# Small tiles in a pool of their own, ahead of the large ones, in a two-layer hybrid decoder

## The chip, the core and the metric

The kernel runs on one core of one Trainium2 chip. The time is the device time of one execution in microseconds (us). Beside the unprofiled runs there is one profiled execution, from which all views of the trace come. TensorE (PE) multiplies matrices and has a weight-load side of its own (PEld); VectorE (DVE), ScalarE (ACT) and GpSimd (POOL) do elementwise work; SyncE (SP) issues all DMAs. SBUF is the on-chip memory in which all operands lie; a tile has the same start address in each of its 128 partitions, and that start, in bytes, is what this case is about.

## The reference

Two decoder layers over x of 1024 positions x 1024 channels, float32. Cut to what matters:

```python
h = rms_norm(x, pre_mix_norm)
proj = h @ w_in                       # 1024 x 3206
o_diff = diff_attention(rope(dq), rope(dk), dv, lam)   # 4 heads, dense causal
o_dil = dilated_attention(rope(lq), rope(lk), lv)      # 6 heads, 3 dilated patterns
o_ssd = ssd_mixer(z, silu(conv4(xbc)), dt, ...)        # 6 heads, chunked scan
x = x + rms_norm(concat(o_diff, o_dil, o_ssd) @ w_out, post_mix_norm)
h = rms_norm(x, pre_ffn_norm)
u = causal_dwconv(h @ ffn_up, width 3)                 # 1024 x 5632
g, val = split(u)
x = x + rms_norm((silu(g) * val) @ ffn_down, post_ffn_norm)
lam = exp(sum(l0 * l1)) - exp(sum(l2 * l3)) + lambda_init   # one number a layer
```

## The kernel before

All large products are made in three passes of a reduced fp32 form (fp32r): each operand is split into a high part and a low part, and high x high, high x low and low x high are added up in PSUM. Positions are taken in two halves T of 512. Every dense matmul has a stationary operand of 128 x 128 and a moving operand of 128 x 512, so 512 columns stream through the array for each.

There are two ways round:

- `mm3` (lines 203, 206, 207): the weights are stationary (a 128-column slice of `wh` or `wl`, the high and low part of a weight tile) and the activations move (a 512-column slice of `ah` or `al`, the high and low part of the normalised input). It makes the input projection by channel and the FFN's up-projection. 1952 matmuls a line.
- `tm3` (lines 153, 156, 157): the activations are stationary and the weights move. They are `ah`/`al` in the token-major input projection and the output projection (512 a line), and the gated FFN tiles tagged `g` in the down-projection (704 a line).

`wsplit` (line 128) loads a weight tile `wr` by DMA, POOL makes `wh` from it (line 134) and DVE makes `wl` (line 135). PSUM results are moved out by ACT and DVE (conv at 359 and 361, FFN gate 812 to 820, sums 840). Attention (score line 593, transposes 733, values 743) and the SSD scan are woven between the dense matmuls; a scheduler lays each engine's order down from the order of the code and the priorities in `weave` and `follow`.

SBUF tiles come from pools, which are laid behind one another; within a pool, the slots of each tag lie in the order in which the tags are first used. Before, there is `cp` (constants `kc` and `gtr`) and one pool `sp` for everything else. A few small tiles (`cstate` of 112 bytes, `ustate` of 352) come first in `sp`, more of them (`tiny`, `rs_m`, `cs`, `sm`, `nA`, `lt`, `wd`) stand between the large ones, and each shifts what follows. At the start of a layer `layer_constants` (line 300) loads small parameters and works out lambda with a handful of tiny instructions (lines 312 to 320).

Of the kernel before, what the change touches and what calls it, by code (L numbers as in the profile page):

```python
# [22 lines left out]
KT = 8  # L23
# [34 lines left out]

C_GPRE, C_GFFN, C_GOUT = 0, 8, 16
C_SSD = 24  # L60
C_FFN = C_SSD + 35
C_TOT = C_FFN + 176
# [7 lines left out]
def body(ctx, tc, x_in, win, wtm, wdt, wout, wup, wdn, cst, gains, dtb, alog, lamp, kst, rope, out):  # L70
    nc = tc.nc
    P = 128
    cp = ctx.enter_context(tc.tile_pool(name="cp", bufs=1))
    sp = ctx.enter_context(tc.tile_pool(name="sp", bufs=2))
    ps = ctx.enter_context(tc.tile_pool(name="ps", bufs=2, space=PSUM))
    dp = ctx.enter_context(tc.tile_pool(name="dp", bufs=2, space=DRAM))

    V, A, G, T_, Y = nc.vector, nc.scalar, nc.gpsimd, nc.tensor, nc.sync

    kc = cp.tile([P, K_GT], F32, name="kc")  # L80
    gtr = cp.tile([P, P], F32R, name="gtr")
    ident = kc[:, K_ID:K_ID + P]
    tri = kc[:, K_TRI:K_TRI + P]
    gts = gtr[:].bitcast(F32)
    sel = kc[:, K_SEL:K_SEL + 8]
# [16 lines left out]
    def tiny(n=4):  # L102
        return sp.tile([P, 8], F32, tag="tiny", bufs=18, name="tiny")

# [3 lines left out]
    def rstd(ssq, n, scale, eps):  # L108
        m = sp.tile([P, 8], F32, tag="rs_m", bufs=4, name="rs_m")
        r = sp.tile([P, 8], F32, tag="rs_r", bufs=4, name="rs_r")  # L110
        m2 = sp.tile([P, 8], F32, tag="rs_2", bufs=4, name="rs_2")
        q = sp.tile([P, 8], F32, tag="rs_q", bufs=4, name="rs_q")
# [184 lines left out]
    for l in range(NL):  # L297
        lam_init = 0.8 - 0.6 * math.exp(-0.3 * l)
        def layer_constants():
            cs = sp.tile([P, C_TOT], F32, tag="cs", bufs=1, name="cs")  # L300
            Y.dma_start(cs[:], cst[l])
            sw = cs[:, C_SSD:C_SSD + 35].rearrange("p (j c) -> p j c", j=7)
            fw = cs[:, C_FFN:C_FFN + 176].rearrange("p (j c) -> p j c", j=44)
            V.tensor_scalar(cs[:, C_SSD:C_SSD + 35], cs[:, C_SSD:C_SSD + 35], 0.5, None, op0=ALU.mult)
            V.tensor_scalar(cs[:, C_FFN:C_FFN + 88], cs[:, C_FFN:C_FFN + 88], 0.5, None, op0=ALU.mult)
            V.tensor_scalar(cs[:, C_GOUT:C_GOUT + 2], cs[:, C_GOUT:C_GOUT + 2], 1.0 - lam_init, None, op0=ALU.mult)
            sm = sp.tile([P, 182], F32, tag="sm", bufs=1, name="sm")
            Y.dma_start(sm[:, 0:24], dtb[l])
            Y.dma_start(sm[:, 24:48], alog[l])
            Y.dma_start(sm[:, 48:182], lamp[l])  # L310
            nA = sp.tile([P, 24], F32, tag="nA", bufs=1, name="nA")
            A.activation(nA[:], sm[:, 24:48], AF.Exp)
            V.tensor_scalar(nA[:], nA[:], -1.0, None, op0=ALU.mult)
            lt = sp.tile([P, 72], F32, tag="lt", bufs=1, name="lt")
            lv = sm[:, 48:176].rearrange("p (a b d) -> p a b d", a=2, b=2)
            V.tensor_tensor(lt[:, 0:64].rearrange("p (a d) -> p a d", a=2), lv[:, :, 0], lv[:, :, 1], op=ALU.mult)
            V.tensor_reduce(lt[:, 64:66], lt[:, 0:64].rearrange("p (a d) -> p a d", a=2), axis=AX.X, op=ALU.add)
            A.activation(lt[:, 66:68], lt[:, 64:66], AF.Exp)
            V.tensor_tensor(lt[:, 68:69], lt[:, 67:68], lt[:, 66:67], op=ALU.subtract)
            V.tensor_scalar(lt[:, 69:70], lt[:, 68:69], -lam_init, None, op0=ALU.add)  # L320
            nlam = lt[:, 69:70]
            wd = sp.tile([P, KT, 12], F32R, tag="wd", bufs=1, name="wd")
# [20 lines left out]
        hT = [None, None]  # L343
        cstate = sp.tile([P, 7, 4], F32, tag="cst", bufs=1, name="cstate")
        ustate = sp.tile([P, 44, 2], F32, tag="ust", bufs=1, name="ustate")
        ropeT = {}
# [75 lines left out]
        dtv = [None, None]  # L422
        ahi = [None, None]

        def dt_unit(T):
            a = acc()
            r = rhs_of(hT[T])
# [10 lines left out]
            w = t2("cv", 4)[:, :192].rearrange("p (a n) -> p a n", a=8)  # L438
            v = sp.tile([P, 24 * 6], F32, tag=f"dtv{T}", bufs=1, name="dtv")
            b = [w[:, i] for i in range(8)]  # L440
# [13 lines left out]
            V.scalar_tensor_tensor(v[:, 0:24], b[3], 2.0, b[0], op0=ALU.mult, op1=ALU.add)  # L454
            V.tensor_tensor(v[:, 24:48], v[:, 0:24], nA[:], op=ALU.mult)
            ah = sp.tile([P, 24], F32R, tag="adt", bufs=2, name="adt")
            ahi[T] = fr(ah[:])
# [3 lines left out]
            p = tr()  # L461
# [7 lines left out]
        prev = [None]  # L469

        def ssd(T, dest=None):
            v = dtv[T]
# [20 lines left out]
            for c in range(4):  # L493
# [5 lines left out]
                ath = t2("P", 4, F32R, n=1024)  # L499
                atl = t2("P", 4, F32R, n=1024)  # L500
# [4 lines left out]
                for j in range(3):  # L505
# [20 lines left out]
                for q in range(2):  # L526
                    sg = tr("s", "s")
                    T_.matmul(sg[:, :384], gtr[:], ath[:, q * 384:(q + 1) * 384], start=True, stop=False)
                    T_.matmul(sg[:, :384], gtr[:], atl[:, q * 384:(q + 1) * 384], start=False, stop=True)
                    A.activation(L[:, q * 384:(q + 1) * 384], sg[:, :384], AF.Exp)  # L530
# [4 lines left out]
                                op=ALU.mult)  # L535
# [356 lines left out]
        if l == 0:  # L892
# [35 lines left out]
        else:  # L928
            cs, sw, fw, sm, nA, nlam, wd = layer_constants()
# [89 lines left out]
def layout(i):  # L1019
# [57 lines left out]
```

## Time and profile before

| what | value |
|---|---|
| unprofiled runs | 2770.76, 2771.83, 2777.04 us; median 2771.83 |
| profiled execution, its own time | 2768.88 us |
| its span, first to last instruction | 2767.2 us |
| mean granted TensorE clock | 0.992 |
| PE / PEld / DVE / ACT / POOL busy | 97 / 77 / 67 / 32 / 26 % of the span |
| DMA engines' packets | 42.6 % of 16 engines' span |

A matmul's busy time in these rows includes the time until its last column has left the array, so neighbours overlap: 1952 matmuls of 403 ns on line 203 are not 787 us of the span. What one matmul costs in a dense stretch is the distance from its start to the next one's start, and that is read from the timeline: first start, last start, number of steps between.

### The profile page before, as it was taken

The numbers are of one execution on the slowest core, as the hardware profiler recorded it, in microseconds if no ns is written. First come the engines' busy times: TensorE is split into PE (matmuls) and PEld (weight loads), VectorE is DVE, ScalarE is ACT, GpSimd is POOL, SyncE is SP. The second block draws the span as 40 slices with busy tenths as digits, with TensorE's granted clock in tenths as the row PEclk, the third lists the DMA queues.
The fourth block names the chain that finished last, engine by engine and source line by source line (L and its number), as shares of the span: only waits on it lengthen the run. The fifth ranks groups of instructions, "written<-read, shape, count | busy, mean of one in ns | idle before, by whom it ended". The sixth has DMA issues, their size and how long they took to land.

```text
span 2767.2 us, 36447 instructions
## 1 busy us (share of the span) xinstructions
PE 2682.0 (97%) x13160; PEld 2142.9 (77%) x13160; DVE 1863.7 (67%) x3814; ACT 882.9 (32%) x1777; POOL 718.7 (26%) x634
## 2 busy tenths in 40 slices
PE   7999989999999999999999999899999999999998
PEld 6787677888778877888877776778887888778886
DVE  5666767556877586566675677675578775956666
ACT  3252333434432232111223533334444222321111
POOL 2301343222123222222133013332221331322222
PEclk9999999999999999999999999999999999999999
DMA  6653545343333444323247535453344334533322
GB/s 224 215 168 101 178 144 181 111 118 111 107 124 116 128 165 153 97 92 96 90 166 231 151 98 191 126 175 111 111 120 131 105 110 128 202 108 98 92 92 69
DMA packets 157348, 368.84 MB, mean 133 GB/s; under 512 B 18032, under 2 KB 53744, under 8 KB 157168
## 3 DMA queue, kind: packets, MB, share of 16 engines
q1 hardware_dynamic: 157168, 366.51, 42.6%
q8 instruction: 105, 1.72, 0.3%
q14 instruction: 75, 0.61, 0.1%
HBM read 306.15 MB, written 60.29 MB: 132 GB/s over the span
## 4 chain that ended last, share of the span: by engine, by line
PE 81%; DVE 10%; issue 5%; POOL 2%; ACT 1%; DMA 1%; SPq 0%; POOLq 0%; DVEq 0%; ACTq 0%
PE acc L203 15%; PE acc L207 15%; PE acc L206 15%; PE acc L156 8%; PE acc L153 8%; PE acc L157 8%; PE po L743 3%; PE s L593 3%; PE tr L733 3%; DVE wl L135 2%; POOL rs_r L114 1%; DVE P L242 1%; PE tr L251 1%; PE tr L552 1%; DVE fT L840 1%
## 5 line engine op out<-in xcount | busy, mean ns | idle before, releaser
L134 POOL TENSOR_SCALAR wh<-wr 128x1024 fp32r<-128x1024 f32 (+1 forms) x390 | 461.7, 1186 | 1428.7 <-PE acc L206 707.7
L203 PE MATMUL acc<-ah,wh 128*128 128x512 f32 x1952 | 785.8, 403 | 1.5 <-ACT ah L254 1.5
L206 PE MATMUL acc<-al,wh 128*128 128x512 f32 x1952 | 775.7, 397 | 0.5 <-DVE al L255 0.5
L207 PE MATMUL acc<-ah,wl 128*128 128x512 f32 x1952 | 775.3, 397 | 0.0
L135 DVE TENSOR_TENSOR wl<-wr,wh 128x1024 fp32r<-128x1024 f32 (+1 forms) x390 | 479.9, 1234 | 285.6 <-POOL wh L134 283.0
L203 PEld LDWEIGHTS acc<-ah,wh 128*128 128x128 f32 x1952 | 368.5, 189 | 92.0 <-issue 10.0
L207 PEld LDWEIGHTS acc<-ah,wl 128*128 128x128 f32 x1952 | 368.4, 189 | 87.2 <-issue 0.7
L206 PEld LDWEIGHTS acc<-al,wh 128*128 128x128 f32 x1952 | 368.5, 189 | 85.0 <-issue 2.7
L361 DVE SCALAR_TENSOR_TENSOR cv<-acc,cs,cv 128x511 f32<-128x511 f32 (+2 forms) x436 | 323.7, 743 | 13.9 <-ACT cv L359 12.6
L359 ACT ACTIVATE cv<-acc,cs 128x512 f32<-128x512 f32 x204 | 158.4, 776 | 426.2 <-PE acc L207 415.5
L153 PE MATMUL acc<-wh,g 128*128 128x512 f32 x704 | 285.1, 406 | 4.7 <-DVE cv L367 4.2
L156 PE MATMUL acc<-wl,g 128*128 128x512 f32 x704 | 280.8, 400 | 6.7 <-DVE rs_m L113 6.7
L157 PE MATMUL acc<-wh,g 128*128 128x512 f32 x704 | 278.6, 399 | 0.0
L595 DVE CUSTOM_DVE_ANT_0 P<-s,kc 128x512 f32<-128x512 f32 (+3 forms) x224 | 130.1, 587 | 158.4 <-PE s L593 152.5
L598 ACT ACTIVATE P<-P,tiny 128x128 f32<-128x128 f32 (+7 forms) x224 | 173.3, 774 | 154.9 <-DVE tiny L597 131.8
L156 PE MATMUL acc<-wl,ah 128*128 128x512 f32 x512 | 205.3, 401 | 16.1 <-DVE wl L135 16.1
L153 PE MATMUL acc<-wh,ah 128*128 128x512 f32 x512 | 205.1, 402 | 4.1 <-POOL wh L134 2.8
L157 PE MATMUL acc<-wh,al 128*128 128x512 f32 x512 | 204.2, 399 | 1.5 <-DVE al L255 1.5
L153 PEld LDWEIGHTS acc<-wh,g 128*128 128x128 f32 x704 | 133.4, 189 | 41.9 <-issue 9.1
L156 PEld LDWEIGHTS acc<-wl,g 128*128 128x128 f32 x704 | 133.7, 190 | 36.9 <-DVE wl L135 7.9
L157 PEld LDWEIGHTS acc<-wh,g 128*128 128x128 f32 x704 | 133.5, 190 | 32.4 <-DVE g L820 1.4
L840 DVE TENSOR_TENSOR fT<-acc,fT 128x512 f32<-128x512 f32 x160 | 108.4, 684 | 73.6 <-PE acc L157 73.4
(183 smaller groups left out, 3151.5 us busy)
## 6 DMA issues: line engine op xcount, KB each, us to landing
wr<-in_wup SPq DMA_DIRECT2D x176, 512.0 KB, 3.5
wr<-in_wdn SPq DMA_DIRECT2D x80, 512.0 KB, 3.5
wr<-in_win SPq DMA_DIRECT2D x54, 512.0 KB, 4.5
wr<-in_wtm SPq DMA_DIRECT2D x32, 512.0 KB, 4.8
wr<-in_wout SPq DMA_DIRECT2D x32, 512.0 KB, 3.9
xd<-t SPq DMA_DIRECT2D x24, 512.0 KB, 2.9
t<-xd SPq DMA_DIRECT2D x24, 512.0 KB, 4.6
t<-in_x SPq DMA_DIRECT2D x16, 512.0 KB, 5.4
```

The source lines that it names most:

```text
L134: G.tensor_scalar(hi[:, :nk * P], raw[:, :nk * P], 1.0, 0.0, op0=ALU.mult, op1=ALU.add)
L135: E_["lo"].tensor_tensor(lo[:, :nk * P], raw[:, :nk * P], fr(hi[:, :nk * P]), op=ALU.subtract)
L153: i = T_.matmul(a[:], xh, hi[:, w], start=(n0 + k == 0), stop=False)
L156: T_.matmul(a[:], xh, lo[:, w], start=False, stop=False)
L157: lastmm[0] = T_.matmul(a[:], xl, hi[:, w], start=False, stop=(n0 + k == n - 1))
L203: i = T_.matmul(a[:], hi[:, w], xh, start=(k == 0), stop=False)
L206: T_.matmul(a[:], hi[:, w], xl, start=False, stop=False)
L207: i = T_.matmul(a[:], lo[:, w], xh, start=False, stop=(k == nk - 1))
L359: A.activation(u[:], a[:], AF.Identity, scale=w[:, n:n + 1], bias=w[:, taps:taps + 1])
L361: V.scalar_tensor_tensor(u[:, d:], a[:, :H - d], w[:, n - d:n - d + 1], u[:, d:], op0=ALU.mult, op1=ALU.add)
L598: A.activation(p[:, :nk * P], p[:, :nk * P], AF.Exp, scale=scale, bias=nm[:, e], accum_out=den[:, e])
L840: V.tensor_tensor(f[t][:, d], a[:], f[t][:, d], op=ALU.add)
```

## The change

A new pool `ss` stands between `cp` and `sp` and takes all small tiles and the 384-column tiles `y` and `prev`. To make the whole fit, `tiny` has 16 slots instead of 18, the unused columns `C_GPRE` and `C_GFFN` of the constants go (`cs` has 219 columns instead of 235), `nA` is made in place in `sm`, and the work tile `lt` becomes a slot of the tag `cv` plus a small tile `ln`. The code of all other work is the same.

```diff
+    ss = ctx.enter_context(tc.tile_pool(name="ss", bufs=2))
     sp = ctx.enter_context(tc.tile_pool(name="sp", bufs=2))
...
-        return sp.tile([P, 8], F32, tag="tiny", bufs=18, name="tiny")
+        return ss.tile([P, 8], F32, tag="tiny", bufs=16, name="tiny")
...
-            nA = sp.tile([P, 24], F32, tag="nA", bufs=1, name="nA")
-            A.activation(nA[:], sm[:, 24:48], AF.Exp)
-            V.tensor_scalar(nA[:], nA[:], -1.0, None, op0=ALU.mult)
-            lt = sp.tile([P, 72], F32, tag="lt", bufs=1, name="lt")
+            nA = sm[:, 24:48]
+            A.activation(nA, nA, AF.Exp)
+            V.tensor_scalar(nA, nA, -1.0, None, op0=ALU.mult)
+            lt = t2("cv", 4)
+            ln = ss.tile([P, 8], F32, tag="lt", bufs=1, name="ln")
...
-            V.tensor_reduce(lt[:, 64:66], lt[:, 0:64].rearrange("p (a d) -> p a d", a=2), axis=AX.X, op=ALU.add)
-            A.activation(lt[:, 66:68], lt[:, 64:66], AF.Exp)
+            V.tensor_reduce(ln[:, 0:2], lt[:, 0:64].rearrange("p (a d) -> p a d", a=2), axis=AX.X, op=ALU.add)
+            A.activation(ln[:, 2:4], ln[:, 0:2], AF.Exp)
...
-        cstate = sp.tile([P, 7, 4], F32, tag="cst", bufs=1, name="cstate")
-        ustate = sp.tile([P, 44, 2], F32, tag="ust", bufs=1, name="ustate")
+        cstate = ss.tile([P, 7, 4], F32, tag="cst", bufs=1, name="cstate")
+        ustate = ss.tile([P, 44, 2], F32, tag="ust", bufs=1, name="ustate")
...
-                nv = sp.tile([P, 384], F32, tag="prev", bufs=2, name="prev")
+                nv = ss.tile([P, 384], F32, tag="prev", bufs=2, name="prev")
```

Where the tiles start, in bytes modulo 512, as the two programs lay them out (slices that the matmuls take lie at multiples of 512 bytes within their tile, so a slice has its tile's offset):

| tiles | before | after |
|---|---|---|
| `ah`, `al`, `fT`, `ptb` (tag act), `t`/`k`/`cxa` (tag K), `gb`, `P` | 192 | 0 |
| `wr`, `wh`, `wl`, `cv` | 256 | 0 |
| `g`, `Q`, `vv`, `pt`/`xdt` | 160 | 0 |
| `on`, `y`, `prev` (first slots) | 480 | 0 |
| `kc`, `gtr` (pool `cp`) | 128, 224 | 128, 224 |

The order of instructions is the same on PE and POOL; on SP only the size of the `cs` load differs. On DVE and ACT the lambda instructions move, in both layers. On DVE at the start of layer 0, after the load of the constants (`cs`, `sm`; `al` is the low part of the second half's input), there stands before:

```order
L306 TENSOR_SCALAR cs<-cs 128x2
L313 TENSOR_SCALAR nA<-nA 128x24
L316 TENSOR_TENSOR lt<-sm 128x64
L317 TENSOR_REDUCE lt<-lt 128x2
L319 TENSOR_TENSOR lt<-lt 128x1
L320 TENSOR_SCALAR lt<-lt 128x1
L255 TENSOR_TENSOR al<-tr,ah 128x4x128 x2
```

and now, where lines have moved down by one or two:

```order
L307 TENSOR_SCALAR cs<-cs 128x2
L314 TENSOR_SCALAR sm<-sm 128x24
L256 TENSOR_TENSOR al<-tr,ah 128x4x128 x2
...
L136 TENSOR_TENSOR wl<-wr,wh 128x1024 x3
L318 TENSOR_TENSOR cv<-sm 128x64
L319 TENSOR_REDUCE ln<-cv 128x2
L321 TENSOR_TENSOR ln<-ln 128x1
L322 TENSOR_SCALAR ln<-ln 128x1
L917 CAST gtr<-cv 128x128
```

Four small instructions have moved behind three weight splits, to just before the copy of `gtr`. On ACT at the same place, the exponential of the lambda sums stands before between two evacuations of the token-major projection's first column half (`cv<-acc` 128x512):

```order
L312 ACTIVATE nA<-sm 128x24
L772 ACTIVATE cv<-acc 128x512
L318 ACTIVATE lt<-lt 128x2
L772 ACTIVATE cv<-acc 128x512
L254 ACTIVATE ah<-tr 128x4x128 x2
```

and now after the last of them, ahead of the first evacuation of the second column half:

```order
L240 ACTIVATE P,tiny<-t_388 128x1024
L774 ACTIVATE cv<-acc 128x512
L320 ACTIVATE ln<-ln 128x2
L776 ACTIVATE cv<-acc 128x384
L777 ACTIVATE cv<-acc 128x128
```

The exponential has moved behind two more evacuations. In layer 1 the same instructions move from the middle of layer 0's work to the end of its FFN. What waits for what is otherwise unchanged: fewer slots of `tiny` alter no wait.

## Rows read from the trace of the kernel before

**Rows 1.** The page: busy time, share of the span, instructions of an engine.
```profile
PE 2682.0 (97%) x13160; PEld 2142.9 (77%) x13160; DVE 1863.7 (67%) x3814; ACT 882.9 (32%) x1777; POOL 718.7 (26%) x634
```

**Rows 2.** The page: the chain that ended last, share of the span by engine, by line.
```profile
PE 81%; DVE 10%; issue 5%; POOL 2%; ACT 1%; DMA 1%; SPq 0%; POOLq 0%; DVEq 0%; ACTq 0%
PE acc L203 15%; PE acc L207 15%; PE acc L206 15%; PE acc L156 8%; PE acc L153 8%; PE acc L157 8%; PE po L743 3%; PE s L593 3%; PE tr L733 3%; DVE wl L135 2%; POOL rs_r L114 1%; DVE P L242 1%; PE tr L251 1%; PE tr L552 1%; DVE fT L840 1%
```

**Rows 3.** Groups by form: line, engine, tiles, shapes, count | busy us, mean ns | idle before.
```profile
L203 PE MATMUL acc<-ah,wh 128*128 128x512 f32 x1952 | 785.8, 403 | 1.5 <-ACT ah L254 1.5
...
L207 PE MATMUL acc<-ah,wl 128*128 128x512 f32 x1952 | 775.3, 397 | 0.0
...
L156 PE MATMUL acc<-wl,g 128*128 128x512 f32 x704 | 280.8, 400 | 6.7 <-DVE rs_m L113 6.7
L156 PE MATMUL acc<-wl,ah 128*128 128x512 f32 x512 | 205.3, 401 | 16.1 <-DVE wl L135 16.1
```

**Rows 4.** Windows: stretch, length and busy us by engine, granted clock, DMA share, GB/s.
```profile
22.95:28.22 5.27, 5.27 (x25) 4.33 (x24) 3.48 (x11) 0.80 (x2) 0.00 (x0) 1.00 0.59 158
1085.57:1099.57 14.00, 14.00 (x62) 11.23 (x61) 7.64 (x10) 2.79 (x4) 3.91 (x3) 1.00 0.34 113
1137.47:1149.37 11.90, 11.90 (x53) 9.58 (x51) 5.82 (x8) 0.00 (x0) 2.88 (x2) 1.00 0.27 88
```

**Rows 5.** Timeline of PE, 22.95 to 28.22 us: start, length, instruction.
```profile
22.95 0.39 PE L153 MATMUL acc<-wh,ah 128*128 128x512 f32 x1
...
28.22 0.40 PE L157 MATMUL acc<-wh,al 128*128 128x512 f32 x1
```

**Rows 6.** Timeline of PE, 1085.57 to 1099.57 us.
```profile
1085.57 0.39 PE L203 MATMUL acc<-ah,wh 128*128 128x512 f32 x1
...
1099.57 0.39 PE L203 MATMUL acc<-ah,wh 128*128 128x512 f32 x1
```

**Rows 7.** Timeline of PE, 1137.47 to 1149.37 us.
```profile
1137.47 0.39 PE L153 MATMUL acc<-wh,g 128*128 128x512 f32 x1
...
1149.37 0.39 PE L153 MATMUL acc<-wh,g 128*128 128x512 f32 x1
```

**Rows 8.** Groups by form: weight loads of the down-projection and of the token-major projections.
```profile
L156 PEld LDWEIGHTS acc<-wl,g 128*128 128x128 f32 x704 | 133.7, 190 | 36.9 <-DVE wl L135 7.9 <-issue 0.7
...
L156 PEld LDWEIGHTS acc<-wl,ah 128*128 128x128 f32 x512 | 97.0, 189 | 42.1 <-DVE wl L135 22.6 <-issue 0.3
```

**Rows 9.** Groups by form: DVE and ACT on tiles `cv` and `g`.
```profile
L816 DVE TENSOR_TENSOR cv<-cv 128x512 f32<-128x512 f32 x88 | 60.4, 687 | 1.2
L812 ACT ACTIVATE cv<-cv 128x512 f32<-128x512 f32 x88 | 55.5, 631 | 204.6 <-DVE cv L367 134.9 <-DVE ustate L364 31.6 <-DVE tiny L597 16.2
...
L402 ACT ACTIVATE g<-g 128x512 fp32r<-128x512 f32 x40 | 23.6, 623 | 79.4 <-DVE g L397 78.6 <-DVE tiny L710 0.4 <-issue 0.4
...
L398 DVE TENSOR_TENSOR g<-g 128x512 f32<-128x512 f32 x20 | 13.6, 678 | 0.0
```

**Rows 10.** The page: DMA queue (packets, MB, share of 16 engines' span).
```profile
q1 hardware_dynamic: 157168, 366.51, 42.6%
```

**Rows 11.** Timeline of DVE at the lambda instructions and where they go.
```profile
25.68 0.22 DVE L316 TENSOR_TENSOR lt<-sm 128x64 f32<-128x64 f32 x1
25.93 0.22 DVE L317 TENSOR_REDUCE lt<-lt 128x2 f32<-128x64 f32 x1
26.42 0.16 DVE L319 TENSOR_TENSOR lt<-lt 128x1 f32<-128x1 f32 x1 [0.27 <-ACT lt L318]
26.62 0.15 DVE L320 TENSOR_SCALAR lt<-lt 128x1 f32<-128x1 f32 x1
29.77 1.29 DVE L255 TENSOR_TENSOR al<-tr,ah 128x512 fp32r<-128x512 f32 x2 [3.00 <-ACT ah L254]
...
48.90 1.07 DVE L915 CAST gtr<-cv 128x128 fp32r<-128x128 f32 x1 [1.53 <-DMA cv<-in_kst]
```

**Rows 12.** Timeline of ACT: the evacuation behind which the exponential now stands.
```profile
52.74 0.49 ACT L774 ACTIVATE cv<-acc 128x384 f32<-128x384 f32 x1 [8.24 <-PE acc L157]
```

More of the change, by code (lines that the diff above doesn't have):

```diff
@@ L56, in in_columns @@
     return np.concatenate([cols[n] for n in IN_ORDER])
-C_GPRE, C_GFFN, C_GOUT = 0, 8, 16
-C_SSD = 24
+C_GOUT = 0
+C_SSD = 8
 C_FFN = C_SSD + 35
@@ L83, in body @@
     tri = kc[:, K_TRI:K_TRI + P]
-    gts = gtr[:].bitcast(F32)
+    gts = gtr[:, :P].bitcast(F32)
     sel = kc[:, K_SEL:K_SEL + 8]
@@ L108, in rstd @@
     def rstd(ssq, n, scale, eps):
[L109 to L112, printed above, removed]
+        m = ss.tile([P, 8], F32, tag="rs_m", bufs=4, name="rs_m")
+        r = ss.tile([P, 8], F32, tag="rs_r", bufs=4, name="rs_r")
+        m2 = ss.tile([P, 8], F32, tag="rs_2", bufs=4, name="rs_2")
+        q = ss.tile([P, 8], F32, tag="rs_q", bufs=4, name="rs_q")
         V.tensor_scalar(m[:, :n], ssq, scale, eps, op0=ALU.mult, op1=ALU.add)
@@ L299, in layer_constants @@
         def layer_constants():
-            cs = sp.tile([P, C_TOT], F32, tag="cs", bufs=1, name="cs")
+            cs = ss.tile([P, C_TOT], F32, tag="cs", bufs=1, name="cs")
             Y.dma_start(cs[:], cst[l])
@@ L306, in layer_constants @@
             V.tensor_scalar(cs[:, C_GOUT:C_GOUT + 2], cs[:, C_GOUT:C_GOUT + 2], 1.0 - lam_init, None, op0=ALU.mult)
-            sm = sp.tile([P, 182], F32, tag="sm", bufs=1, name="sm")
+            sm = ss.tile([P, 182], F32, tag="sm", bufs=1, name="sm")
             Y.dma_start(sm[:, 0:24], dtb[l])
@@ L310, in layer_constants @@
             Y.dma_start(sm[:, 48:182], lamp[l])
-            nA = sp.tile([P, 24], F32, tag="nA", bufs=1, name="nA")
-            A.activation(nA[:], sm[:, 24:48], AF.Exp)
-            V.tensor_scalar(nA[:], nA[:], -1.0, None, op0=ALU.mult)
-            lt = sp.tile([P, 72], F32, tag="lt", bufs=1, name="lt")
+            nA = sm[:, 24:48]
[3 more added lines that the diff above has]
+            ln = ss.tile([P, 8], F32, tag="lt", bufs=1, name="ln")
             lv = sm[:, 48:176].rearrange("p (a b d) -> p a b d", a=2, b=2)
             V.tensor_tensor(lt[:, 0:64].rearrange("p (a d) -> p a d", a=2), lv[:, :, 0], lv[:, :, 1], op=ALU.mult)
-            V.tensor_reduce(lt[:, 64:66], lt[:, 0:64].rearrange("p (a d) -> p a d", a=2), axis=AX.X, op=ALU.add)
-            A.activation(lt[:, 66:68], lt[:, 64:66], AF.Exp)
[L319 to L322, printed above, removed]
+            V.tensor_reduce(ln[:, 0:2], lt[:, 0:64].rearrange("p (a d) -> p a d", a=2), axis=AX.X, op=ALU.add)
+            A.activation(ln[:, 2:4], ln[:, 0:2], AF.Exp)
+            V.tensor_tensor(ln[:, 4:5], ln[:, 3:4], ln[:, 2:3], op=ALU.subtract)
+            V.tensor_scalar(ln[:, 5:6], ln[:, 4:5], -lam_init, None, op0=ALU.add)
+            nlam = ln[:, 5:6]
+            wd = ss.tile([P, KT, 12], F32R, tag="wd", bufs=1, name="wd")
             wdr = t2("cv", 4)[:, :48].rearrange("p (a n) -> p a n", a=KT)
@@ L438, in dt_unit @@
             w = t2("cv", 4)[:, :192].rearrange("p (a n) -> p a n", a=8)
-            v = sp.tile([P, 24 * 6], F32, tag=f"dtv{T}", bufs=1, name="dtv")
+            v = ss.tile([P, 24 * 6], F32, tag=f"dtv{T}", bufs=1, name="dtv")
             b = [w[:, i] for i in range(8)]
@@ L454, in dt_unit @@
             V.scalar_tensor_tensor(v[:, 0:24], b[3], 2.0, b[0], op0=ALU.mult, op1=ALU.add)
-            V.tensor_tensor(v[:, 24:48], v[:, 0:24], nA[:], op=ALU.mult)
-            ah = sp.tile([P, 24], F32R, tag="adt", bufs=2, name="adt")
+            V.tensor_tensor(v[:, 24:48], v[:, 0:24], nA, op=ALU.mult)
+            ah = ss.tile([P, 24], F32R, tag="adt", bufs=2, name="adt")
             ahi[T] = fr(ah[:])
@@ L511, in ssd @@
                                 xdt[:, 0, :384].rearrange("p (h d) -> p h d", h=6), b6(col(3, c), 64), op=ALU.mult)
-                xD = sp.tile([P, 384], F32, tag="y", bufs=3, name="y")
+                xD = ss.tile([P, 384], F32, tag="y", bufs=3, name="y")
                 V.tensor_tensor(xD[:].rearrange("p (h d) -> p h d", h=6),
@@ L527, in ssd @@
                     sg = tr("s", "s")
-                    T_.matmul(sg[:, :384], gtr[:], ath[:, q * 384:(q + 1) * 384], start=True, stop=False)
-                    T_.matmul(sg[:, :384], gtr[:], atl[:, q * 384:(q + 1) * 384], start=False, stop=True)
+                    T_.matmul(sg[:, :384], gtr[:, :P], ath[:, q * 384:(q + 1) * 384], start=True, stop=False)
+                    T_.matmul(sg[:, :384], gtr[:, :P], atl[:, q * 384:(q + 1) * 384], start=False, stop=True)
                     A.activation(L[:, q * 384:(q + 1) * 384], sg[:, :384], AF.Exp)
@@ L544, in ssd @@
                                   start=(g == 0), stop=(g == 1))
-                    ys = sp.tile([P, 384], F32, tag="y", bufs=3, name="ys")
+                    ys = ss.tile([P, 384], F32, tag="y", bufs=3, name="ys")
                     V.tensor_tensor(ys[:].rearrange("p (h d) -> p h d", h=6),
@@ L568, in ssd @@
                 ssq = tiny()
-                yq = sp.tile([P, 384], F32, tag="y", bufs=3, name="yq")
+                yq = ss.tile([P, 384], F32, tag="y", bufs=3, name="yq")
                 for g in range(2):
@@ L914, in body @@
             Y.dma_start(gt0[:, :P], kst[:, K_GT:])
-            V.tensor_copy(gtr[:], gt0[:, :P])
+            V.tensor_copy(gtr[:, :P], gt0[:, :P])
             cs, sw, fw, sm, nA, nlam, wd = layer_constants()
@@ L1037, in chan @@
         return a.reshape(NL, -1, 128).transpose(0, 2, 1)
-    c[:, :, C_GPRE:C_GPRE + 8] = chan(f["pre_mix_norm"])
-    c[:, :, C_GFFN:C_GFFN + 8] = chan(f["pre_ffn_norm"])
     c[:, :, C_GOUT:C_GOUT + 2] = chan(np.tile(f["diff_head_norm"], (1, 4)))
```

## The prediction

> **What bounds the kernel now.** First the busy times: TensorE is busy for 97% of the span, 2682.0 us, and no other engine for more than 67% [rows 1]. Then the chain that ended last: 81% of it is TensorE, and 69% of it the six lines of the dense matmuls, 45% `mm3` (lines 203, 206, 207) and 24% `tm3` (153, 156, 157) [rows 2]. The time is therefore the pitch of these matmuls, from one start to the next, times their number. A change that moves no TensorE instruction can show in the time mainly through that pitch, or through what TensorE waits for: DVE 10%, POOL 2%, ACT 1%, DMA 1% of the chain.
>
> The mean of about 400 ns in the groups by form [rows 3] is not the pitch: matmuls overlap. The pitch is read from a stretch in which TensorE has no gap, as the distance between two far starts over the number of steps; in the windows [rows 4] two of the instructions counted are one that still runs at the start and one that begins at the end, so there are two steps fewer than instructions. All three stretches have a granted clock of 1.00, which is 2.4 GHz.
> - `tm3` on `ah`/`al`, from 22.95 to 28.22 us [rows 5]: 5.27 us over 23 steps, 229.1 ns.
> - `mm3`, from 1085.57 to 1099.57 [rows 6]: 14.00 us over 60 steps, 233.3 ns.
> - `tm3` on `g`, from 1137.47 to 1149.37 [rows 7]: 11.90 us over 51 steps, 233.3 ns.
>
> At 2.4 GHz these are 550, 560 and 560 ticks for 512 columns; one column per tick would be 213.3 ns.
>
> This is the reading on which the forecast stands. The first and third stretch have one shape, one number form and one moving tile; they differ in the stationary tile, `ah` against `g`. It isn't contention: the stretch that is faster has the busier VectorE (3.48 of 5.27 us against 5.82 of 11.90) and the busier DMA (0.59 against 0.27) [rows 4]. It isn't the weight load either, 189 and 190 ns [rows 8]. What does differ is where the operand starts: `ah` at 192 bytes modulo 512, a multiple of 64, and `g` at 160, which isn't one. In `mm3` the moving tile is the one at 192, in `tm3` it is at 256. One rule fits all three: a stationary operand off a multiple of 64, or a moving operand off a multiple of 128 or 256, costs 10 ticks, 4.2 ns. That is an inference from three pairs of offsets. After the change all of these operands start at 0.
>
> **The change part by part.**
>
> *Offsets of the dense operands.* The step is 233.3 - 229.1 = 4.2 ns. I take it only for matmuls on the chain, since the rest of the time TensorE waits for others.
> - `mm3`: 45% of 2767.2 us is 1245 us; over 0.2333 that is 5337 of the 5856 matmuls (three lines of 1952 [rows 3]). Gain 5337 x 4.2 ns = 22.4 us.
> - `tm3`: 24% is 664 us. By count, `g` has 704 of 1216 a line [rows 3], 58%: 384 us, 1647 matmuls. Gain 6.9 us.
> - `tm3` on `ah`: the other 280 us, 1222 matmuls, stays at 229.1 ns.
>
> The sum is 29.3 us. From both sides: nothing, if offsets aren't the cause; at the other end all that stands above 213.3 ns, 20.0 ns on 5337 + 1647 matmuls and 15.8 on 1222, which is 139.7 + 19.3 = 159 us; below nothing, the same step of 4.2 ns the other way on each of 8206 matmuls, 34.5 us lost. I take 29.3, because only 229.1 has been seen in this kernel, and the ends for the range.
>
> *Offsets of the attention operands.* The scores (line 593) are 3% of the chain, 83 us [rows 2]; the same 1.8% of it (4.2 of 233.3) would be 1.5 us. Their short runs give no clean pitch; I take nothing, with 0 to 2 us gained.
>
> *Offsets on VectorE and ScalarE.* `cv` lies at 256 and `g` at 160 today. On VectorE 128x512 takes 687 ns on `cv` and 678 on `g`; on ScalarE 631 and 623 [rows 9]. The tile at the worse offset isn't slower, so nothing; these engines are 11% of the chain, and 1% of that would be 3 us either way.
>
> *Offsets of DMA targets.* 366.51 MB move in 157168 packets [rows 10], most of it into `wr`, from 256 to 0. The trace has no DMA into one tile at two offsets. DMA is 1% of the chain, 28 us; a tenth of it, 3 us either way, is my bound, and I take nothing.
>
> *Lambda.* Four instructions of 0.15 to 0.22 us leave VectorE at 25.68 to 26.77 us, 1.1 us with their waits, and 3.00 us of idle follow there; where they now stand, ahead of line 915 at 48.90, VectorE has 1.53 us idle, waiting for a DMA, and the four need 0.75 us busy [rows 11]. If that idle were gone, the copy of `gtr` would be up to 1.1 us later, and so twice over both layers 2.2 us. ScalarE's exponential now stands ahead of an evacuation with 8.24 us of idle before it [rows 12]. The new VectorE instructions wait for that exponential, and behind them are the copy of `gtr` and the SSD's work, which run while TensorE still has the projection's next columns. Nothing.
>
> *Fewer `tiny` slots, `cs` smaller, `nA` in place.* The waits stay as they are; nothing.
>
> Sum against the profiled execution: 2768.88 - 29.3 = 2739.6 us. Its span is 2767.2, so 1.7 us lie around it, and they stay. The median of the runs is 2771.83, 2.95 above the profiled execution: 2742.5, said as 2743.
>
> **A rule against it.** The trace has two pitches, 229.1 and 233.3 ns, for tiles whose offsets are all multiples of 32 bytes [rows 5, 7]. The Trainium skill, "SBUF — State Buffer", section "Specifications (TRN2)", gives SBUF lines of 16 bytes, with a price for each crossing to a new one. By that a run of 512 neighbouring values crosses as often from any of these offsets, so the change would give nothing: rival 1. The pair of pitches speaks against it by 4.2 ns, though it isn't proof.
>
> **The rivals.**
>
> 1. *Start addresses aren't the cause.* `g` differs from `ah` in more than its offset: another writer, another distance between its tiles. Then nothing that the change does reaches the pitch, and the time is 2772. For it: three pairs of offsets carry the rule, and today's kernel has no operand at 0. Against it: shape, clock and moving tile are the same, and `mm3` and `tm3` on `g` land on the same 560 ticks with different writers. Chance 0.19.
>
> 2. *More goes than has been seen.* 229.1 is still 37 ticks above 512; if that too is offset (192 stationary, 256 moving), all of it could go: 2772 - 159 = 2613, or with half of it about 2690. For it: no pair of operands at 0 is in the trace. Against it: 550 and 560 are two neat levels, and a third one is a guess. Chance 0.10. The Trainium skill, "TensorE: Matmul & The Clock Gate", section "Back-to-back issue gap", measures 512 columns over 2.4 GHz plus about 2.5 ns, for bf16; an estimate by that page, 17.5 ns on 6984 matmuls and 13.3 on 1222, would be 138 us gained. No row here comes near that pitch.
>
> 3. *Equal offsets collide* (the other side). Today the stationary and the moving operand differ by 64 bytes (192 and 256) or 96 (160 and 256) modulo 512; none agree. After the change both start at 0, the weight load of the next matmul runs beside the moving reads of this one (TensorE's load side is busy 77% of the span [rows 1]), and if what counts is the distance between the two, each of 8206 matmuls goes up: with one more step of 4.2 ns, 34.5 us, 2806. It turns slower as soon as the collision costs more than the 3.6 ns (29.3 us over 8206) that alignment gives. For it: `ah` with `wh` has one pitch when `wh` moves and another when `wh` stands, so the pair matters and not the tile. Against it: distances of 64 and 96 give the same 560 ticks. Chance 0.10.
>
> 4. *Only the stationary side counts*, and 233.3 in `mm3` has another cause: the gain is 6.9 us, 2765. For it: the cleanest pair differs in the stationary tile alone. Against it: two causes for one level. Chance 0.09. (That only the moving side counts gives 22.4, 2749, and lies in my own range.)
>
> **How the numbers follow.** My forecast, 2743, has 0.52; its own range is 2735 to 2755 (the 3 us of DMA, the 3 us of VectorE and ScalarE, the 2.2 of lambda and 2 of attention, and either term of the sum at two thirds). The rivals have 0.19, 0.10, 0.10 and 0.09. This kernel's runs can tell a change of about 0.2%, 5.5 us. Faster by more: 0.52 + 0.10 + most of rival 4, 0.70. Within: rival 1 and the rest of 4, 0.20. Slower: rival 3, 0.10. The range leaves out rival 3 and the larger half of rival 2, and reaches from 2700 to 2776.
>
> **What would show it.** Right: in `mm3` and in `tm3` on `g`, starts 229 ns apart (60 steps in 13.75 us in place of 14.00), `tm3` on `ah` unchanged, TensorE's busy time down by some 30 us, and DVE, ACT and weight loads with the durations of today. A pitch of 233.3 left in `mm3` alone is rival 4; in both, rival 1; below 229 anywhere, rival 2; above 233.3, rival 3. Were the pitch down but the time not, TensorE would wait more, for VectorE's weight splits at line 135 first (2% of the chain). The forecast is wrong outside 2735 to 2755.

## The result, and the profile after

The changed kernel took 2745.48 us (median of four runs, 2741.57 to 2747.96) against 2774.43 beside it, a ratio of 0.9895 with an interval of 0.9875 to 0.9914: 29 us faster. 2743 had been forecast. Timed once more beside the kernel before, it took 2742.26 against 2776.25, ratio 0.9881 (0.9868 to 0.9895): 33 us. The time came out as forecast, but by other steps: the pitch fell by more than forecast and for another reason, and a part of that didn't reach the time.

The pitch first. Windows of the changed kernel, of `tm3` on `ah`, of `mm3` and of `tm3` on `g`; the columns are those of [rows 4]:

```profile
39.34:44.14 4.80, 4.80 (x23) 3.94 (x21) 4.13 (x7) 0.00 (x0) 4.04 (x4) 1.00 0.61 217
1079.23:1092.84 13.61, 13.61 (x62) 11.27 (x61) 7.57 (x10) 2.79 (x4) 3.97 (x4) 1.00 0.35 116
1129.33:1140.89 11.56, 11.56 (x53) 9.57 (x52) 6.32 (x8) 0.00 (x0) 2.92 (x2) 1.00 0.29 90
```

and the starts in them, on the timeline of TensorE:

```profile
39.34 0.39 PE L154 MATMUL acc<-wh,ah 128*128 128x512 f32 x1
...
44.13 0.39 PE L154 MATMUL acc<-wh,ah 128*128 128x512 f32 x1
...
1079.23 0.39 PE L204 MATMUL acc<-ah,wh 128*128 128x512 f32 x1
...
1092.83 0.39 PE L204 MATMUL acc<-ah,wh 128*128 128x512 f32 x1
...
1129.33 0.39 PE L157 MATMUL acc<-wl,g 128*128 128x512 f32 x1
...
1140.88 0.39 PE L154 MATMUL acc<-wh,g 128*128 128x512 f32 x1
```

There are two steps fewer than instructions counted. (Further down some counts are one lower, because the last start lies just past the window's edge; there the number of steps is given.) This gives: `tm3` on `ah` 4.79 us over 21 steps, 228.1 ns (229.1 in [rows 5]); `mm3` 13.60 over 60, 226.7 (233.3 in [rows 6]); `tm3` on `g` 11.55 over 51, 226.5 (233.3 in [rows 7]). Over all undisturbed steps of the trace the means are 228.0, 227.5 and 228.0 ns, against 229.5, 233.3 and 233.5. At 2.4 GHz, 226.7 ns are 544 ticks.

Weight loads take 189 to 194 ns (189 and 190 in [rows 8]). The page gives TensorE 33.0 us less busy time than [rows 1], VectorE 21 more:

```profile
PE 2649.0 (97%) x13160; PEld 2147.8 (78%) x13160; DVE 1885.0 (69%) x3814; ACT 883.0 (32%) x1777; POOL 721.5 (26%) x634
```

The lambda instructions cost nothing that the trace shows. VectorE's timeline where they now stand in layer 0 (compare [rows 11]): the idle time before the copy of `gtr` is 0.41 us in place of 1.53, and it still ends with a DMA. In layer 1 they run from 1341.7 to 1350.9 us, and TensorE's matmuls go on beside them without a gap.

```profile
48.50 0.16 DVE L321 TENSOR_TENSOR ln<-ln 128x1 f32<-128x1 f32 x1 [0.27 <-ACT ln L320]
48.70 0.15 DVE L322 TENSOR_SCALAR ln<-ln 128x1 f32<-128x1 f32 x1
49.27 1.07 DVE L917 CAST gtr<-cv 128x128 fp32r<-128x128 f32 x1 [0.41 <-DMA cv<-in_kst]
```

### The profile page after: what moved, and what is told of

The parts are those of the page before. It is cut to its first block, busy times and chain, and to the rows that moved or that the text cites. A ratio compares the mean times of both kernels' runs of the same rounds, so it can differ in the third digit from the quotient of the medians.

```text
span 2743.9 us, 36451 instructions
## 1 busy us (share of the span) xinstructions
PE 2649.0 (97%) x13160; PEld 2147.8 (78%) x13160; DVE 1885.0 (69%) x3814; ACT 883.0 (32%) x1777; POOL 721.5 (26%) x634
## 5 line engine op out<-in xcount | busy, mean ns | idle before, releaser
L204 PE MATMUL acc<-ah,wh 128*128 128x512 f32 x1952 | 776.3, 398 | 1.5 <-ACT ah L255 1.5
L207 PE MATMUL acc<-al,wh 128*128 128x512 f32 x1952 | 765.8, 392 | 0.5 <-DVE al L256 0.5
L208 PE MATMUL acc<-ah,wl 128*128 128x512 f32 x1952 | 764.7, 392 | 0.0
```

The lines of the kernel that those rows point to most:

```text
L204: i = T_.matmul(a[:], hi[:, w], xh, start=(k == 0), stop=False)
L207: T_.matmul(a[:], hi[:, w], xl, start=False, stop=False)
L208: i = T_.matmul(a[:], lo[:, w], xh, start=False, stop=(k == nk - 1))
```

## The experiments

Distances below are the start of the moving operand minus that of the stationary one, modulo 256 bytes. Before, they were 192 (`mm3`, 192 - 256), 64 (`tm3` on `ah`, 256 - 192) and 96 (`tm3` on `g`, 256 - 160); after, all 0.

**Each operand's own offset, or the distance between the two?** A kernel of bursts alone:

```python
m = {o: sp.tile([P, H + 8], F32R, tag="m%d" % o) for o in range(0, 512, 32)}   # moving, at o
s = {o: sp.tile([P, P + 8], F32R, tag="s%d" % o) for o in range(0, 512, 32)}   # stationary, at o
def burst(so, mo, n=20, sx=0, mx=0):
    for i in range(n):
        T_.matmul(a[:], s[so][:, sx:sx + P], m[mo][:, mx:mx + H], start=(i == 0), stop=(i == n - 1))
```

> Not the decoder: it leaves out both layers and copies x to the output; in front of that, TensorE runs bursts of 20 matmuls of the dense shape (stationary 128x128 fp32r, moving 128x512 fp32r), one pair of start offsets per burst: stationary at 0 with the moving operand at 0, 32, ..., 480 modulo 512; moving at 0 with the stationary one at 32, ..., 480; some pairs of the decoder before; then all again in reverse order, and three shifts of 4, 8 and 16 bytes. No DMA and little else runs beside them. Theory A (each operand has an alignment of its own): pair 0/0 about 227 ns, the pace of the changed decoder; moving at 192 about 233 with any stationary offset; stationary at 160 with moving at 0 or 256 about 233; and the pitch follows from the two offsets one by one. Theory B (only the distance of the two operands counts): 64/64, 160/160, 192/192 and 256/256 give the pitch of 0/0, and (0, 192) that of (256, 448 or 64). Theory C (offsets don't count, what ran beside the matmuls or where they were in memory did): one pitch within 0.5 ns for all pairs.

Five of its bursts, 19 steps each: moving 256 on stationary 0; moving 0 on stationary 192; moving 256 on stationary 160; moving 192 on stationary 256; both at 160.

```profile
58.99:63.31 4.32, 4.32 (x21) 3.57 (x19) 0.00 (x0) 0.60 (x1) 0.00 (x0) 1.00 0.00 0
119.45:123.81 4.36, 4.36 (x21) 3.57 (x20) 0.00 (x0) 0.60 (x1) 0.00 (x0) 1.00 0.00 0
170.50:174.93 4.43, 4.43 (x21) 3.57 (x19) 0.00 (x0) 0.60 (x1) 0.00 (x0) 1.00 0.02 4
184.29:188.72 4.43, 4.43 (x20) 3.55 (x19) 0.00 (x0) 0.60 (x1) 0.00 (x0) 1.00 0.00 0
193.63:197.94 4.31, 4.31 (x20) 3.57 (x19) 0.00 (x0) 0.60 (x1) 0.00 (x0) 1.00 0.00 0
```

227, 229, 233, 233 and 227 ns. A pair at 160 is as fast as a pair at 0 or 256: an offset of its own costs nothing, among multiples of 32. The pairs whose offsets are multiples of 32 fall into one table by distance. It gives the lowest and highest mean of a pair's two bursts, without their first step:

| distance | 0 | 32 | 64 | 96 | 128 | 160 | 192 | 224 |
|---|---|---|---|---|---|---|---|---|
| pitch, ns | 226.7 to 227.5 | 233.0 to 233.3 | 228.9 to 229.2 | 233.3 to 233.8 | 232.8 to 233.1 | 234.1 to 234.4 | 233.1 to 233.3 | 232.8 to 233.3 |

One pair is left out at 64: stationary 448 with moving 0 had 229 ns in its first burst and 233.3 in its second, so one pair can hold either pace, and what chooses is not known. Three shifts of one operand by 4, 8 and 16 bytes, also in this run, bound the theory. With the stationary operand moved up by 4 bytes the distance is 252, and the pitch 232.5 ns; the next run has the same distance, made by the moving operand, at 227.4. By 8 bytes (distance 248) the two agree, 230.6 and 230.4; by 16 (distance 240) they don't, 233.1 against 236.2. The second burst of 448/0, then the stationary operand at 4:

```profile
244.32:248.75 4.43, 4.43 (x20) 3.59 (x19) 0.00 (x0) 0.60 (x1) 0.00 (x0) 1.00 0.00 0
388.48:392.90 4.42, 4.42 (x21) 3.56 (x19) 0.00 (x0) 0.60 (x1) 0.00 (x0) 1.00 0.00 0
```

The decoder's three kinds before and after lie in the table. So the theory of the distance holds for offsets that are multiples of 32, and that of own alignment, which was the prediction's, falls. For smaller steps the distance alone doesn't give the pitch.

**A finer grid, and is it the load of the weights?** The same bursts with `m[...][:, mx:mx + H]` moved by 4 bytes at a time, with stationary operands of `w` columns, and with fewer moving columns:

> Not the decoder: it leaves out both layers and copies x to the output; in front of that, TensorE runs bursts of one shape each. First 64 bursts of 20 dense matmuls with the stationary operand at 0 and the moving one at 0, 4, 8, ..., 252 bytes; then stationary operands of 128, 96, 64 and 32 columns with the moving one at 0, 64, 96, 128 and 192; then the moving operand with 256 and 128 columns. Theory B2 (the pitch follows the distance between the two operands modulo 256, because the load of the next weights and the moving reads share something in SBUF): distance 0 gives 226.7 ns and is the lowest or among the lowest of all 64; 64 gives 229, 96 to 224 give 233 to 234; and what stands above 213.3 ns (13.3 at distance 0, 20 at 128 and 192) shrinks with the columns of the stationary operand, to about half at 64 columns and a quarter at 32. Rival (a cost of each matmul, such as its issue, with no part for the load): 13 to 20 ns at every width, and with 256 or 128 moving columns as well. Rival (own alignment of each operand): the moving operand off a multiple of 64 costs the same 4 to 7 ns at every such offset, 4 bytes as well as 32.

Distances 0, 28 and 100 at full width, then distances 0 and 192 with 32 stationary columns:

```profile
21.40:25.71 4.31, 4.31 (x21) 3.57 (x19) 0.00 (x0) 0.60 (x1) 0.00 (x0) 1.00 0.82 291
53.90:58.22 4.32, 4.32 (x20) 3.55 (x19) 0.00 (x0) 0.60 (x1) 0.00 (x0) 1.00 0.02 4
137.42:141.96 4.54, 4.54 (x20) 3.64 (x19) 0.00 (x0) 0.60 (x1) 0.00 (x0) 1.00 0.00 0
388.99:393.39 4.40, 4.40 (x21) 2.07 (x19) 0.00 (x0) 0.59 (x1) 0.00 (x0) 1.00 0.00 0
407.54:411.94 4.40, 4.40 (x21) 2.07 (x19) 0.00 (x0) 0.59 (x1) 0.00 (x0) 1.00 0.02 4
```

Over 64 distances the pitch runs from 226.6 (distance 0) to 239.8 ns (196), mean 233.0. Distances 28, 60, 108, 156 and 252 also stay under 227.5; none is below 226.6. Here own alignment falls again: 28 is as good as 0. But the second half of the expectation failed. The surplus over 213.3 ns doesn't shrink with the stationary columns: with 32 of them the pitch is 231.7 and 231.6 ns at distances 0 and 192, the loads of a burst being busy 2.07 us in place of 3.57. With 96, 64 and 32 columns all pitches lie from 228.2 to 232.9 ns, 15 to 20 above 213.3, and distance 0 is not the lowest. With 256 moving columns the pitch is 117.8 to 119.8 ns, 11 to 13 above one column per tick, and again not lowest at 0; with 128 it is 111.6 to 111.7 without the first steps, 58 above. So the best distance hangs on the shape too, and the lowest pitch isn't a share of the load's length. The rival, a cost of each matmul with no part for the load, fits every width and nearly the 256 moving columns, but not the 128; where the 13.3 ns at distance 0 come from stays open.

**Whose weights, and does other traffic count?** Two pairs of offsets in turn, and bursts with VectorE or DMA work beside:

```python
so, mo = pairs[i % len(pairs)]
T_.matmul(a[:], s[so][:, :P], m[mo][:, :H], start=(i == 0), stop=(i == n - 1))
```

> Not the decoder: it leaves out both layers; in front of a copy of x to the output, TensorE runs bursts of 60 dense matmuls in which two pairs of start offsets take turns, and bursts with VectorE subtractions of 128x1024 or DMA loads of 512 KB beside them. Theory N (what counts is the distance between the moving operand and the weights of the NEXT matmul, which are loaded meanwhile): pairs (0,0),(128,128), written stationary first, have own distance 0 but 128 to the next weights, 233 ns; (0,128),(128,0) have 128 of their own and 0 to the next, 226.7; (0,0),(64,64) alternates 192 and 64, about 231; (0,64),(64,0) is 226.7. Theory O (the distance to its own weights): 226.7 for (0,0),(128,128) and for (0,0),(64,64), 233 for (0,128),(128,0), 231 for (0,64),(64,0). Under both, (0,0),(0,128) and (0,0),(128,0) lie half way, 230. Traffic: the kernel's 227.5 against 226.7 in the earlier bursts would be VectorE's or the DMAs' reads if 0,0 rises by about 1 ns beside one of them; nothing if it stays within 0.3 ns.

Traffic first. Distance 0 alone, with ten VectorE subtractions, with DMA loads, and the same three at distance 128:

```profile
242.77:256.14 13.37, 13.37 (x61) 11.08 (x59) 0.00 (x0) 0.60 (x1) 0.00 (x0) 1.00 0.00 0
256.37:269.74 13.37, 13.37 (x61) 11.08 (x59) 12.14 (x11) 0.60 (x1) 0.00 (x0) 1.00 0.00 1
283.57:296.94 13.37, 13.37 (x61) 11.08 (x59) 0.00 (x0) 0.60 (x1) 0.00 (x0) 1.00 0.06 21
310.77:324.53 13.76, 13.76 (x61) 11.08 (x59) 0.00 (x0) 0.60 (x1) 0.00 (x0) 1.00 0.00 1
324.76:338.53 13.77, 13.77 (x61) 11.08 (x59) 12.54 (x11) 0.60 (x1) 0.00 (x0) 1.00 0.00 0
352.76:366.53 13.77, 13.77 (x61) 11.08 (x59) 0.00 (x0) 0.60 (x1) 0.00 (x0) 1.00 0.14 57
```

13.37 us over 59 steps whatever runs beside, and 13.76 or 13.77. So VectorE's traffic costs nothing here, nor do DMAs at 21 and 57 GB/s; the decoder's stretches above have 88 to 217 GB/s, and ScalarE and GpSimd were not tried.

The other half settles nothing. (0,0),(128,128) gave 228.4 ns, steps of 226.7 and 230.0 in turn; (0,128),(128,0) 230.0; (0,0),(64,64) 231.7; (0,64),(64,0) 233.2. The next weights should have made them 233, 226.7, 231 and 226.7, the own weights 226.7, 233, 226.7 and 231. Neither fits all four. Both theories put (0,0),(0,128) and (0,0),(128,0) at 230; the first gave 230.0, the second 233.1. Which reads meet is open.

**All large tiles at 192.** One unused tile of 192 bytes ahead of all large ones:

```diff
+    sp.tile([128, 48], F32, tag="pad0", bufs=1, name="pad0")
```

> The changed kernel with 192 unused bytes ahead of all large tiles: all of them start at 192 modulo 512, at distance 0 from each other. Distance theory: pitch of 227.5 ns in all six dense lines as in the changed kernel, time 2745 within 0.2%. Own alignment (the prediction's reading): moving operands at 192 cost, mm3 at 233.3 and tm3 at 229 to 233, 5337 x 5.8 = 31 us and up to 16 more, 2776 to 2792.

2742.67 us, ratio to the kernel before 0.9879 (0.9864 to 0.9894): as fast as the changed kernel. `mm3`, 60 steps:

```profile
1079.40:1093.00 13.60, 13.60 (x62) 11.26 (x60) 7.56 (x10) 2.79 (x4) 3.98 (x4) 1.00 0.36 116
```

226.7 ns with the moving operand at 192, where it had 233.3 before. The distance decides in the decoder too, and the multiple of 512 in the change's description is not needed.

**`ah`, `al` at 64, everything from `wr` on at 256.** Two such tiles, of 64 bytes at the start and of 192 ahead of `wr`:

```diff
+    sp.tile([128, 16], F32, tag="pad0", bufs=1, name="pad0")
...
+        if "w" not in E_:
+            E_["w"] = sp.tile([P, 48], F32, tag="pad1", bufs=1, name="pad1")
```

> The changed kernel with ah, al, fT, the attention's K tiles, gb and P at 64 modulo 512 and all from wr on at 256. Distance theory: mm3 (moving minus stationary 64 modulo 256) 229 ns, tm3 on ah (192) 233, tm3 on g (0) 227.5; 5337 x 1.5 + 1222 x 5.8 = 15 us over the changed kernel, 2760. Own alignment: mm3 with its moving operand at 64, off a multiple of 128, 233.3, tm3 on ah with the stationary operand on a multiple of 64 at 229 or less: 31 + 2 = 33 us, 2778.

2755.87 us, ratio 0.9925 (0.9912 to 0.9937), 13 us over the kernel with all at 192. `tm3` on `ah` (21 steps) and `mm3` (60):

```profile
40.66:45.56 4.90, 4.90 (x22) 3.95 (x21) 4.23 (x7) 0.00 (x0) 4.09 (x4) 1.00 0.60 224
1081.05:1094.80 13.75, 13.75 (x61) 11.27 (x60) 7.59 (x10) 2.79 (x4) 3.99 (x4) 1.00 0.34 115
```

233.3 and 229.2 ns: against the kernel before, the two kinds have changed places, since 64 and 192 have. Own alignment had 2778.

**`ah`, `al` at 192, everything from `wr` on at 256:** the same edit with 192 and 64 bytes. Of the dense matmuls it puts only those on `g` right; the rest of the change (lambda, slots, the offsets of `Q`, `vv` and others) is in it too.

> The changed kernel with ah, al, fT, the attention's K tiles, gb and P at 192 modulo 512 and all from wr on at 256: the kernel before with g alone put right. Both theories: mm3 233.3, tm3 on ah 229, tm3 on g 227.5. What it tells is how much of the pitch reaches the time: 5337 x 5.8 + 1222 x 1.4 = 33 us over the changed kernel, 2778, if all of it does; some 2765 to 2770 if a third is given back in waits and in a lower clock, as between the two profiles.

2774.44 us, ratio 0.9991 (0.9981 to 1.0). `mm3`, then `tm3` on `g`:

```profile
1089.88:1103.88 14.00, 14.00 (x62) 11.22 (x61) 7.65 (x10) 2.79 (x4) 3.96 (x4) 1.00 0.33 113
1141.09:1152.65 11.56, 11.56 (x52) 9.57 (x51) 6.33 (x8) 0.00 (x0) 2.93 (x2) 1.00 0.28 90
```

233.3 and 226.7 ns as expected, and 32 us over the kernel at 192, about all of the pitch (33). But against the kernel before, the term of `g`, 9 us by its pitch, shows as 0 to 5.

**`g` alone put wrong.** 160 bytes ahead of `g`:

```diff
+        if tag == "g" and "g" not in E_:
+            E_["g"] = sp.tile([P, 40], F32, tag="pad2", bufs=1, name="pad2")
```

> The changed kernel with 160 unused bytes ahead of g: g, Q, vv, pt and on start at 160 modulo 512, all before them at 0 as in the changed kernel. tm3 on g has distance 96 again, 233.3 ns, and mm3 and tm3 on ah stay at 227.5. If the 5.4 ns reach the time on the 1647 matmuls that were counted on the chain, 8.8 us over the changed kernel; act192 against the kernel before gave 2.0 for the same term, with an interval of 0 to 5 us, and if that is the true size TensorE waits for g's weights or for the conv that much longer when it is faster, 2 to 4 us.

2751.48 us, ratio 0.9916 (0.9903 to 0.9928), 9.2 us over the changed kernel beside it: all of the term. `tm3` on `g` in it:

```profile
1133.51:1145.41 11.90, 11.90 (x52) 9.58 (x51) 6.33 (x8) 0.00 (x0) 2.87 (x2) 1.00 0.27 88
```

So the same 6.6 ns a step are worth 9 us between two forms of the changed kernel, and about 2 against the kernel before. The intervals, some 3 us each, leave room for a smaller difference. Part of it goes with the clock: the 11 runs with `ah` at 192 have a mean granted clock of 0.9885, the 42 runs of the kernel before whose clock is on record 0.9897, and in those 42 a clock lower by 0.001 comes with a time longer by some 2 us. The rival is a cost of a few us in the rest of the change, which is in this kernel and not in the kernel before. The changed kernel was never run with all the old distances, so it is not excluded.

**Both kernels once more,** unchanged, to see how far one profile can be trusted:

> The kernel before, unchanged, for a second profile of it. Its first profile took 2768.88 us at a mean granted clock of 0.992; other runs of it lay at 0.989 and 2775 to 2778. Theory G (the gain of the pitch is partly given back in a lower clock that the change causes): this profile again has clock drops at about the places of the first one, 37 us of half clock before the last drop. Rival (the first profile was a run with few drops, and the kernel before drops as often as the changed one): drops at 340 to 400 and 1660 to 1780 us as in the changed kernel, 50 to 65 us of half clock, 2776 us.

> The changed kernel, unchanged, timed beside the kernel before on the same chip. If the whole of the pitch's gain reaches the time, 31 + 9 + 2 = 42 us less than before; by the first comparison 29 (2745.5 against 2774.4); a third given back in waits and clock gives 28 to 33.

The kernel before took 2776.59 us (median of 11 runs), the changed one 2742.26. Span and mean granted clock of the four profiles, first pair (before, after), then second pair:

```profile
core 0: 2767.2 us, clock 0.992
```

```profile
core 0: 2743.9 us, clock 0.988
```

```profile
core 0: 2772.8 us, clock 0.991
```

```profile
core 0: 2738.4 us, clock 0.990
```

The first pair is 23.3 us apart, the second 34.4. By the record of the granted clock, the kernel before spent 37 us at half clock (1.2 GHz) in its first profile and 44 in its second, the changed one 61 and 48 (all but the drop at the very end). One such place, from 300 to 400 us, in the first pair:

```profile
300.00:400.00 100.00, 89.67 (x474) 70.63 (x474) 76.58 (x173) 37.91 (x102) 42.78 (x33) 1.00 0.54 173
```

```profile
300.00:400.00 100.00, 88.90 (x451) 70.46 (x451) 73.15 (x154) 35.68 (x94) 40.29 (x31) 0.95 0.52 164
```

The second profile of the kernel before drops there too:

```profile
300.00:400.00 100.00, 89.36 (x455) 70.09 (x453) 74.70 (x168) 36.86 (x100) 42.10 (x33) 0.97 0.53 168
```
So the first pair overstates what the change costs in clock: the kernel before lies between 0.988 and 0.993 over its 42 runs, and its first profile was at the upper end. A small loss isn't excluded. The changed kernel's eight runs have a mean of 0.9885 against 0.9897, which by the 2 us above would be some 2.5 us, an estimate.

The second pair is the one to account with. Windows of four stages, cut beside the same GpSimd instructions (within 0.3 us); before:

```profile
495.91:987.76 491.85, 491.26 (x2672) 398.27 (x2670) 331.35 (x723) 184.61 (x353) 125.54 (x114) 1.00 0.39 117
...
1077.44:1463.95 386.51, 382.06 (x1670) 307.51 (x1669) 243.90 (x383) 76.92 (x123) 89.45 (x78) 1.00 0.34 109
...
1832.81:2323.64 490.83, 490.26 (x2680) 397.80 (x2679) 342.59 (x741) 185.43 (x349) 129.46 (x114) 1.00 0.41 121
...
2408.55:2772.78 364.23, 352.34 (x1506) 281.89 (x1505) 230.42 (x372) 69.33 (x109) 82.94 (x71) 0.99 0.31 97
```

and after:

```profile
490.86:976.03 485.17, 483.71 (x2671) 397.97 (x2670) 332.19 (x719) 184.53 (x352) 126.83 (x114) 1.00 0.39 118
...
1064.68:1444.18 379.50, 374.89 (x1670) 308.17 (x1669) 251.25 (x387) 76.84 (x124) 90.66 (x78) 1.00 0.35 112
...
1811.65:2296.76 485.11, 482.73 (x2677) 397.01 (x2676) 345.89 (x741) 185.51 (x349) 128.24 (x114) 1.00 0.41 122
...
2381.96:2738.37 356.41, 343.04 (x1504) 281.01 (x1502) 236.83 (x372) 69.39 (x109) 83.37 (x71) 0.99 0.31 99
```

The FFN stages (second and fourth), nearly all dense, lose 7.0 of 386.5 and 7.8 of 364.2 us; those with attention in between (first and third) 6.7 of 491.9 and 5.7 of 490.8. Over the whole span TensorE is busy 2686.5 us before and 2644.1 after, 42.4 less, and idle 86.3 and 94.3, 8.0 more: 34.4 us remain.

## Why the prediction was right, and where it wasn't

- *What bounds the kernel*: right. The pitch of the dense matmuls fell and the time with it, with the same instructions on TensorE.
- *"One rule fits all three"*: wrong, though it is what the forecast stood on. The stationary operand at a multiple of 64, the moving one at 128 or 256, is not what counts; their distance modulo 256 is, for offsets in steps of 32 (bursts, all at 192, `ah` at 64). From three pairs both readings fit. The prediction wrote down distances of 64 and 96 bytes without their sign: `mm3` has -64, that is 192, and `tm3` on `ah` has +64. With the sign, the three pitches of [rows 4] belong to three different distances, and the argument "distances of 64 and 96 give the same 560 ticks" falls.
- *The step of 4.2 ns*: too small. It took `tm3` on `ah` as the aligned case, and that one was at 64. The step is 5.8 ns for `mm3`, 5.5 for `g` and 1.5 for `ah`, which was to stay: 5337 x 5.8 + 1647 x 5.5 + 1222 x 1.5 = 41.8 us in place of 29.3.
- *What of it lies on the path*: the other error, of nearly the same size and the other way. Counting only the chain's share left out that TensorE, when faster, waits more: idle 8.0 us more, spread over nearly all stages (9.7 in the first pair). 41.8 - 8.0 is 33.8, against 34.4 in the second pair of profiles. This agreement is itself partly luck: 41.8 counts the 8206 matmuls of the chain, all 9504 dense ones would give 47.9, and TensorE's busy time fell by 42.4. That 2743 came out near 2745.48 is two errors that cancel, and runs that vary by their clock.
- *Rival 1* falls: pitch and time follow the start addresses. The rule of the Trainium skill ("SBUF — State Buffer", "Specifications (TRN2)") of lines of 16 bytes does not account for it: by that rule alone, start offsets that are multiples of 32 would all be alike. They are not, 226.7 to 234.4 ns in steps of 32.
- *Rival 2* was a little right: below 229.1 there was more, 2.4 ns of 15.8; 226.6 is the floor of 64 distances.
- *Rival 3* named the right quantity, the distance of the pair, with the wrong sign: equal offsets are the best case of the dense shape.
- *VectorE as today*: wrong, mostly for one line. The gate's low part (line 820, now 822) went from 715 to 885 ns, 15 of VectorE's 21 us; the last section says why.
- *Lambda, DMA, `tiny`*: nothing seen, as said; no run tests them apart from the offsets. That VectorE's weight splits would be late next was too narrow: the idle time that came stands before many instructions, the largest new piece before the first matmul on `g` (wait for `cv`, 5.1 to 7.3 us in the second pair).

## What to carry to other kernels

Read the pitch of a matmul from start to start in a gapless stretch, and where kinds of one shape differ, compare the start addresses of the moving and the stationary tile as a signed difference, modulo 256 bytes, with starts at multiples of 32. With 128 stationary and 512 moving columns of fp32r, matmuls run 3% faster at 0 than at most other distances; with 96 or fewer stationary columns, or 256 moving ones, 0 was not the best. A reading that rests on three pairs is tested cheaply by bursts over all offsets before it is believed. A gain in the pitch of the bounding engine arrives less what the engine then waits, here about a fifth of it, and one pair of profiles can mis-state it by ten microseconds where the clock drops vary.

## What was not expected of the hardware

The pitch depends on the moving operand's start in steps as small as 4 bytes: 226.6, 236.5, 233.0, 228.9 ns at 0, 4, 8 and 12 past the stationary one's.

VectorE's slower line isn't an offset: with `g` at 160 and `cv` at 0 it is 886 ns too, and the median of the 88 stays at 693. 21 of them take over 0.9 us in the second profile after, 19 of these about 1.5, against 2 over 0.9 before. All 21 overlap a GpSimd instruction that started first, 18 of them the making of `wh`. The order of the two starts decides. One and the same instruction, before: VectorE starts first, and GpSimd's instruction is stretched from 1.05 to 1.31 us:

```profile
2486.54 0.69 DVE L820 TENSOR_TENSOR g<-cv,g 128x512 fp32r<-128x512 f32 x1 [0.70 <-ACT g L819]
2486.83 1.31 POOL L134 TENSOR_SCALAR wh<-wr 128x1024 fp32r<-128x1024 f32 x1 [4.55 <-PE acc L206]
```

After, GpSimd, which waits for a matmul to free the weight slot, starts 0.05 us ahead, and VectorE takes 1.53 us:

```profile
2458.54 1.05 POOL L135 TENSOR_SCALAR wh<-wr 128x1024 fp32r<-128x1024 f32 x1 [4.21 <-PE acc L207]
2458.59 1.53 DVE L822 TENSOR_TENSOR g<-cv,g 128x512 fp32r<-128x512 f32 x1 [0.70 <-ACT g L821]
```

Whoever comes second waits for the other. The Trainium skill, "SBUF — State Buffer", section "Terms", says as much: the two engines share a pair of ports, held by one for a whole instruction, and the loser is blocked; these rows agree (0.84 us later for a start 0.05 us too late). That the faster `mm3` brings this about is borne out by the other traces: 21 of 88 are slow in all four with `mm3` at 227 to 228 ns, 5 with it at 229 (`ah` at 64), and 2 or 3 in those with it at 233. What of TensorE's 8 us of idle time comes from this was not separated.
